# Layer 0's second FFN projection in three chunks, the last by column groups, with its weights' low parts on GpSimd

## The chip, the cores and the metric

One core of one Trainium2 chip runs the kernel. The metric is the device time of one execution in microseconds, as the median of several runs. Times inside an execution are counted from its first instruction.

## What is computed

A diffusion trunk of two layers over 256 context and 512 latent tokens (768 columns in all), model width 1024. Layer 0 has a mixer (pooling and a gated recurrence), layer 1 grouped-query attention; each is followed by a SwiGLU FFN with 2816 hidden units. Every sub-layer is wrapped in two RMSNorms and in a modulation (shift, scale, gate) that is computed from the conditioning vectors:

```python
def swiglu(h, w_in, w_out):
    a, b = jnp.split(h @ w_in, 2, axis=-1)
    return (jax.nn.silu(a) * b) @ w_out
...
        f_lat = swiglu(rmsnorm(x, norm_g[l, 2]) * (1.0 + sc2) + sh2, ffn_w_in[l], ffn_w_out[l])
        x = x + g2 * rmsnorm(f_lat, norm_g[l, 3])
...
        h_lat = rmsnorm(x, norm_g[l, 0]) * (1.0 + sc1) + sh1
```

The stretch of the kernel in question is `@ w_out` of layer 0, then its norm and residual (the "postnorm"), then the norm and modulation ahead of layer 1 (the "prenorm"), then the projection to queries and keys of layer 1 with RMSNorm per head and rotary positions.

## The kernel before

**Layout and products.** All activations are feature-major: 128 features in the partitions, tokens along the free axis; width 1024 is 8 tiles of 128. Every 32-bit product is made of three products of rounded parts, high by high, high by low and low by high (`mm3`, L185 to L187). A weight slot of 2048 columns is loaded as 1024-column pieces `raw` by SyncE's queue (L113, a pool of four buffers); ScalarE writes the high part (`whi`, `w3hi`, L641), and VectorE subtracts it to get the low part (`wlo`, `w3lo`, L642).

**The projection** (`ffn0`). The 22 hidden tiles of 128 went to DRAM (`gd`) while the first projection ran, and come back through GpSimd's DMA queue: `g` (L790) and `hh`/`hl` (L806). The 22 tiles are summed in four chunks of 7, 8, 3 and 4 (`FCH`). In the first three the loops run over the 8 output tiles n and, inside, over the column groups 0 to 256 and 256 to 768; the result of a chunk is added to `y` on VectorE (L734; the first chunk is copied by ScalarE, L732). The last chunk of 4 runs over three column groups of 256 instead (256 to 512, 512 to 768, then the context 0 to 256), and inside over n. All seven loads of `g` for the last two chunks, and before them the sixteen of the second chunk, are issued in one go.

**Work alongside.** A generator given to `along` is run in steps by `tick`: the code hands it as many microseconds of credit as the matmuls just written take, and a step costs what the generator yields. So the order of the code on each engine is set by these costs (VectorE, ScalarE and GpSimd run their queues in order). Beside the first three chunks the modulation of layer 1 is computed (`ada_cols`: 24 weight rows `adat`, each loaded as a `raw` and multiplied by the conditioning vector `cb` on VectorE, L366; twice for the first 16 rows). After each column group of the last chunk, `done` is started along the next: `postnorm` and `prenorm`, in steps for each of the 8 feature tiles: squares on ScalarE and their sums on VectorE (`ss`, L232, L233), the sum over partitions by TensorE (`rms`, L204), the power on GpSimd (`rr`, L210), the spread by TensorE (L219), the scaled tile `u` (L294, L249), the addition to `x` on GpSimd (L298), the high and low parts `hh`, `hl` (L256, L257).

**The projection to queries and keys** (`att_proj`) takes these `hh`, `hl`. First four heads of queries on the columns 256 to 512, two heads on 512 to 768, two more there, then both groups of keys, the other queries on 256 to 768, and the context's keys. Per head there is a sum of squares (`sq`, L912), a partition sum (L204), and the rotary positions (`sw`, L883 to L886, partition swaps by DMA). The first attention matmuls (`st`) follow.

Of the kernel before, what the change touches and what calls it, by code (L numbers as in the profile page):

```python
# [15 lines left out]
D = 1024  # L16
# [16 lines left out]
FCH = ((7, 8, 3, 4), (4, 4, 4, 4, 4, 2))  # L33
# [37 lines left out]

class Byg:
# [5 lines left out]
    def add(self, a, src):  # L78
        t = self.t[a // 256] = self.pool.tile([128, KD, 256], F32, tag=self.tag, name=self.tag, bufs=self.bufs)
        self.eng.dma_start(out=t, in_=src[:, :, a:a + 256])  # L80
        return t

    def __call__(self, k, a, b):
        return self.t[a // 256][:, k, a % 256:a % 256 + b - a]

# [7 lines left out]
class Trunk:  # L93
# [30 lines left out]
    def wtile(self, pool=None, tag="w"):  # L124
# [3 lines left out]
        return [pool.tile([128, 2048], F32R, tag=tag + t, name=tag + t) for t in ("hi", "lo")]  # L128
# [131 lines left out]

    def sumsq_all(self, xa):
# [21 lines left out]
    def postnorm(self, x, y, l, which, a, b):  # L283
# [8 lines left out]
        for k in range(KD):  # L292
# [6 lines left out]
            yield 0.75  # L299

# [58 lines left out]
    def ada_cols(self, m):  # L359
# [4 lines left out]
        for i in range(2 if m < 16 else 1):  # L364
            junk = self.rawp.tile([128, 1024], F32, tag="raw", name="junk") if m < 16 and not i else raw
            nc.vector.scalar_tensor_tensor(out=junk, in0=raw, scalar=1.0, in1=self.cb[:, i * 1024:i * 1024 + 1024],  # L366
                                           op0=ALU.mult, op1=ALU.mult, accum_out=self.mods[1][:, m, i:i + 1])
# [3 lines left out]
    def load_cb(self, cb, n):  # L371
        self.cb = cb
        self.nc.sync.dma_start(out=cb, in_=self.a["cb"][:n].partition_broadcast(128))
        self.nc.scalar.activation(out=cb, in_=cb, func=AF.Silu)
# [367 lines left out]
    def ffn0(self, y, h, closed, done, top):  # L742
# [18 lines left out]
        for i, (a, b) in [(i, g) for i in range(3) for g in G3[:2]] + [(i, G3[2]) for i in range(3)]:  # L761
            if a == G3[2][0] and i == 0:
# [4 lines left out]
                self.load_cb(self.tmp.tile([128, 1024], F32, name="cb0"), 1024)  # L767
# [19 lines left out]
        with self.pool("g2", side="right") as gp:  # L787
            def gload(j, k):
                t = gp.tile([128, 2, NT], F32R, tag=f"g{k}", name=f"g{k}")
                nc.gpsimd.dma_start(out=t, in_=gd[j].bitcast(F32R))  # L790
# [10 lines left out]
            with self.pool("cb") as cp:  # L801
                cb = cp.tile([128, 2048], F32, name="cb1")
                gb = self.htiles()
                for k in range(KD):
                    for p in range(2):
                        nc.gpsimd.dma_start(out=gb[p](k, 0, NT), in_=gd[7 + k][:, p, :].bitcast(F32R))  # L806
                g.append(gb)
                for ci in range(3):
                    if ci == 2:
                        ts = [gload(15 + k, k) for k in range(7)]  # L810
                        g += [two(ts[:3]), two(ts[3:])]
# [524 lines left out]
```

## Time and profile before

| | |
|---|---|
| median of 3 runs | 1622.92 us (1621.41 to 1623.31) |
| the profiled execution | 1618.92 us |
| its span, first to last instruction | 1617.2 us |
| TensorE busy in it | 1538.5 us (95%) |
| VectorE / ScalarE / GpSimd busy | 1001.6 / 644.2 / 120.9 us |
| second projection, from its first matmul to the first of the query projection | 768.7 to 962.0 us |
| query and key projection, up to the first `st` | 962.0 to 1067.9 us |
| mean granted TensorE clock | 0.985 of full speed |

The profile lists busy time of each engine, the idle time ahead of groups of instructions and what ended it. Matmuls overlap in the pipeline, so a matmul's own duration is longer than its pitch; times of stretches are read from starts. The median is 4.0 us above the profiled execution.

### The profile page before, as it was taken

Reading aid. Unit: us, or ns where it says so; the run is one execution under the profiler, and the core shown is the slowest. Engines: PE = TensorE matmul, PEld = TensorE weight load, DVE = VectorE, ACT = ScalarE, POOL = GpSimd, SP = SyncE. Lnnn points to the kernel's source line nnn. Section 1 sums busy time; section 2 is a strip of 40 time slices with the busy share of each in tenths; the row PEclk is TensorE's granted clock in tenths of the full one; section 3 lists DMA queues with packets and bytes.
Section 4 is the critical chain, followed back from the end, with each engine's and each line's share of the span. In section 5 each row is a group of like instructions: output and inputs, shape, how many; then the busy total and the mean of one; then the engine's idle time right before and its main releaser. Section 6 shows DMA issues by size and latency. Waiting matters only on the chain.

```text
span 1617.2 us, 26585 instructions
## 1 busy us (share of the span) xinstructions
PE 1538.5 (95%) x10656; PEld 1378.1 (85%) x10656; DVE 1001.6 (62%) x1923; ACT 644.2 (40%) x1228; POOL 120.9 (7%) x166
## 2 busy tenths in 40 slices
PE   5999999999899999999999996999998999999997
PEld 2877777789899999999888896899998988888886
DVE  5466575644779988974367476679947434244345
ACT  3334343254655444443221134458945332222222
POOL 0000000001210000001100022310013000000002
PEclk9999999999999999999999997999999999999999
DMA  9142232342415565536996322230032332332211
GB/s 368 55 157 80 79 128 83 124 134 89 154 64 175 193 194 192 170 127 237 354 319 210 100 87 81 77 97 27 1 118 66 105 101 83 103 104 89 94 53 52
DMA packets 75850, 207.25 MB, mean 128 GB/s; under 512 B 7760, under 2 KB 32848, under 8 KB 75600
## 3 DMA queue, kind: packets, MB, share of 16 engines
q1 hardware_dynamic: 70448, 184.92, 35.1%
q0 software_dynamic: 5136, 20.45, 3.4%
q8 instruction: 83, 1.36, 0.4%
q14 instruction: 39, 0.32, 0.1%
q10 hardware_dynamic: 144, 0.20, 0.0%
HBM read 178.28 MB, written 24.64 MB: 125 GB/s over the span
## 4 chain that ended last, share of the span: by engine, by line
PE 58%; DVE 6%; DMA 5%; ACT 2%; POOL 2%; issue 1%; SPq 0%; POOLq 0%; DVEq 0%; ACTq 0%
PE mm L185 18%; PE mm L186 18%; PE mm L187 18%; DMA gd<-gs 2%; DMA raw<-adat 1%; DVE ss L233 1%; PE pp L1024 1%; DMA raw<-w_fo 1%; POOL x L298 1%; PE aux L204 1%; PE st L185 1%; PE aux L219 1%; PE st L187 1%; PE st L186 1%; DVE wlo L642 1%
## 5 line engine op out<-in xcount | busy, mean ns | idle before, releaser
L185 PE MATMUL mm<-hh,whi 128*128 128x256 f32 (+2 forms) x1292 | 428.6, 334 | 5.0 <-DVE y L734 2.9
L187 PE MATMUL mm<-hh,wlo 128*128 128x256 f32 (+2 forms) x1292 | 425.5, 331 | 1.3 <-issue 1.0
L186 PE MATMUL mm<-hl,whi 128*128 128x256 f32 (+2 forms) x1292 | 425.9, 331 | 0.0
L185 PEld LDWEIGHTS mm<-hh,whi 128*128 128x128 f32 x1292 | 246.3, 192 | 34.9 <-issue 7.7
L187 PEld LDWEIGHTS mm<-hh,wlo 128*128 128x128 f32 x1292 | 246.5, 191 | 19.1 <-issue 1.2
L186 PEld LDWEIGHTS mm<-hl,whi 128*128 128x128 f32 x1292 | 246.7, 191 | 16.6 <-DVE hl L642 0.2
L641 ACT ACTIVATE whi<-raw 128x1024 fp32r<-128x1024 f32 (+2 forms) x145 | 133.9, 945 | 234.4 <-PE mm L186 122.7
L642 DVE TENSOR_TENSOR wlo<-raw,whi 128x1024 fp32r<-128x1024 f32 (+2 forms) x145 | 156.4, 1093 | 58.4 <-ACT whi L641 56.9
L210 POOL TENSOR_TENSOR rr<-rv,mhalf 128x2 f32<-128x2 f32 (+1 forms) x53 | 41.7, 789 | 1096.7 <-DVE rv L207 1078.7
L678 DVE TENSOR_TENSOR sa<-sa,mm 128x256 f32<-128x256 f32 (+2 forms) x38 | 20.7, 546 | 159.1 <-PE mm L187 159.0
L734 DVE TENSOR_TENSOR y<-y,mm 128x256 f32<-128x256 f32 (+1 forms) x104 | 55.9, 542 | 69.4 <-PE mm L187 68.5
L185 PE MATMUL mm<-hh,w3hi 128*128 128x256 f32 (+2 forms) x284 | 93.3, 330 | 2.8 <-ACT w3hi L641 1.4
L187 PE MATMUL mm<-hh,w3lo 128*128 128x256 f32 (+2 forms) x284 | 92.8, 327 | 1.4 <-DVE w3lo L642 1.4
L186 PE MATMUL mm<-hl,w3hi 128*128 128x256 f32 (+2 forms) x284 | 92.9, 328 | 0.0
L641 ACT ACTIVATE w3hi<-raw 128x1024 fp32r<-128x1024 f32 (+2 forms) x51 | 43.2, 876 | 101.7 <-PE mm L186 71.6
L233 DVE TENSOR_TENSOR ss<-ss,sq 128x256 f32<-128x256 f32 x126 | 58.0, 468 | 37.3 <-ACT sq L232 32.1
L366 DVE SCALAR_TENSOR_TENSOR raw<-raw,cb 128x1024 f32<-128x1024 f32 x48 | 58.7, 1222 | 12.4 <-DMA raw<-adat 11.7
L642 DVE TENSOR_TENSOR w3lo<-raw,w3hi 128x1024 fp32r<-128x1024 f32 (+2 forms) x51 | 50.1, 1001 | 16.4 <-ACT w3hi L641 16.4
L185 PEld LDWEIGHTS mm<-hh,w3hi 128*128 128x128 f32 x284 | 53.9, 190 | 6.5 <-ACT q L705 1.7
L187 PEld LDWEIGHTS mm<-hh,w3lo 128*128 128x128 f32 x284 | 53.8, 190 | 4.7 <-DVE w3lo L642 1.6
L186 PEld LDWEIGHTS mm<-hl,w3hi 128*128 128x128 f32 x284 | 53.9, 190 | 3.1
L185 PE MATMUL mm<-g,whi 128*128 128x256 f32 (+1 forms) x176 | 54.5, 310 | 0.0
(294 smaller groups left out, 3354.1 us busy)
## 6 DMA issues: line engine op xcount, KB each, us to landing
raw<-w_fi SPq DMA_DIRECT2D x88, 512.0 KB, 4.3
raw<-ada SPq DMA_DIRECT2D x48, 512.0 KB, 5.3
raw<-adat SPq DMA_DIRECT2D x48, 512.0 KB, 4.3
raw<-w_fo SPq DMA_DIRECT2D x40, 512.0 KB, 4.5
gd<-gs SPq DMA_DIRECT2D x38, 384.0 KB, 2.8
g<-gd POOLq DMA_DIRECT2D x14, 768.0 KB, 11.7
raw<-w_ab SPq DMA_DIRECT2D x20, 512.0 KB, 4.7
x<-x SPq DMA_DIRECT2D x6, 1024.0 KB, 6.9
```

The costliest lines, as they stand in the source:

```text
L185: self.nc.tensor.matmul(out=out, lhsT=wh, rhs=xh, start=first and i == 0, stop=False, **kw)
L186: self.nc.tensor.matmul(out=out, lhsT=wh, rhs=xl, start=False, stop=False, **kw)
L187: self.nc.tensor.matmul(out=out, lhsT=wl, rhs=xh, start=False, stop=i == n - 1, **kw)
L204: nc.tensor.matmul(out=pc[:, 2 * t:2 * t + 2], lhsT=ss[:, t * 128:(t + 1) * 128], rhs=self.ones[:, 0:2], start=True, stop=True)
L210: nc.gpsimd.tensor_tensor(out=r[:, :nt], in0=v[:, :nt], in1=self.mhalf[:, :nt], op=ALU.pow)
L219: nc.tensor.matmul(out=pb[:, t * 128:(t + 1) * 128], lhsT=r[:, t:t + 1].to_broadcast([128, 128]), rhs=self.ident, start=True, stop=True)
L233: nc.vector.tensor_tensor(out=ss[:, :n], in0=ss[:, :n], in1=sq[:, :n], op=ALU.add)
L366: nc.vector.scalar_tensor_tensor(out=junk, in0=raw, scalar=1.0, in1=self.cb[:, i * 1024:i * 1024 + 1024], op0=ALU.mult, op1=ALU.mult, accu ...
L641: self.nc.scalar.activation(out=hi, in_=src, func=AF.Copy)
L642: (eng or self.nc.vector).tensor_tensor(out=lo, in0=src, in1=hi.bitcast(F32), op=ALU.subtract)
L678: nc.vector.tensor_tensor(out=s[:, :n], in0=s[:, :n], in1=p[1][:, :n], op=ALU.mult)
L734: nc.vector.tensor_tensor(out=y(n, a, b), in0=y(n, a, b), in1=pt[:, :b - a], op=ALU.add)
```

## The change

- **Chunks.** 7, 8 and 7 hidden tiles. The first two run as before; the last, now 7 tiles, runs by the three column groups as the chunk of 4 did, with its own packing of weights (`w_fo0c`, 7168 columns in four slots; the fourth in a small pool `we`), and all are loaded before its first group.
- **Loads held.** `fetch` prepares a slot of weights one slot ahead. While it runs, low parts are computed on GpSimd (`weng`). The DMAs that bring `hh`/`hl` of the second chunk, `g` of the third and `x` are issued two tiles (or so) per slot; ahead of each, GpSimd copies two columns of the slot's last low part into the target, so that the DMA cannot start before that low part is there.
- **Modulation.** Rows 0 to 15 run beside the first two chunks, from the fourth output tile on, at a cost of 5.7 (before: all 24 from the fifth, at 5.0); rows 16 to 23 run beside the last chunk at 2.1. `cb` is two tiles of 1024, and the unused product has its own tile `junk` in place of a `raw`.
- **Norms.** `postnorm4` and `prenorm4` work on four feature tiles at once: squares of 128x1024 on ScalarE, sums of 512 columns, the scaling as one 128x1024 instruction from PSUM; the residual addition is one 128x1024 addition on GpSimd for tiles 0 to 3 and four fused multiply-adds on VectorE for tiles 4 to 7.
- **Query and key projection.** Keys of the first latent group follow its four query heads; then four heads of the second group, its keys, heads 4 to 6 on both, the context's keys, and head 7. Squares have their own buffers.

The core of the diff:

```diff
-FCH = ((7, 8, 3, 4), (4, 4, 4, 4, 4, 2))
+FCH = ((7, 8, 7), (4, 4, 4, 4, 4, 2))
...
+    def add(self, a, src, hold=None):
         t = self.t[a // 256] = self.pool.tile([128, KD, 256], F32, tag=self.tag, name=self.tag, bufs=self.bufs)
+        if hold is not None:
+            self.eng.tensor_copy(out=t[:, 0, 0:2], in_=hold)
         self.eng.dma_start(out=t, in_=src[:, :, a:a + 256])
...
+    def sumsq4(self, src, a, b):
+        nc = self.nc
+        ss = self.sm.tile([128, 256], F32, tag="ss", name="ss")
+        for k in (0, 4):
+            sq = self.np.tile([128, 4, 256], F32, tag="sq", name="sq", bufs=1)
+            nc.scalar.activation(out=sq, in_=src.view(a, b, k, k + 4), func=AF.Square)
+            nc.vector.tensor_tensor(out=sq[:, 0:2, :], in0=sq[:, 0:2, :], in1=sq[:, 2:4, :], op=ALU.add)
+            for x, z in ((sq[:, 0, :], sq[:, 1, :]),) if k == 0 else ((ss, sq[:, 0, :]), (ss, sq[:, 1, :])):
+                nc.vector.tensor_tensor(out=ss, in0=x, in1=z, op=ALU.add)
+            yield 1.3
...
+    def scaled(self, out, src, rb, a, b, k):
+        self.nc.vector.tensor_tensor(out=out.view(a, b, k, k + 4), in0=src.view(a, b, k, k + 4),
+                                     in1=rb[:, :b - a].unsqueeze(1).to_broadcast([128, 4, b - a]), op=ALU.mult)
...
+    def postnorm4(self, x, y, l, which, a, b):
...
+        for k0 in (0, 4):
+            self.scaled(y, y, rb, a, b, k0)
+            if k0 == 0:
+                for k in range(k0, k0 + 4):
+                    nc.scalar.activation(out=y(k, a, b), in_=y(k, a, b), func=AF.Copy,
+                                         scale=self.gcol[l][which][:, k, c:c + 1])
+                nc.gpsimd.tensor_tensor(out=x.view(a, b, 0, 4), in0=x.view(a, b, 0, 4), in1=y.view(a, b, 0, 4), op=ALU.add)
+            else:
+                for k in range(k0, k0 + 4):
+                    nc.vector.scalar_tensor_tensor(out=x(k, a, b), in0=y(k, a, b), scalar=self.gcol[l][which][:, k, c:c + 1],
+                                                   in1=x(k, a, b), op0=ALU.mult, op1=ALU.add)
+            yield 3.0
...
+                def fetch():
...
+                    ci, n = nxt.pop(0)
+                    w = wo[ci, n] = self.fo(0, ci, n)
+                    t = w[1][:, 1024:1026].bitcast(F32)
+                    if ci == 0:
+                        for k in (n, n + 1):
+                            for p in range(2):
+                                if n:
+                                    nc.gpsimd.tensor_copy(out=gb[p](k, 0, 2), in_=t)
+                                nc.gpsimd.dma_start(out=gb[p](k, 0, NT), in_=gd[7 + k][:, p, :].bitcast(F32R))
+                    elif n:
+                        for k in range(n - 2, n if n < 6 else 7):
+                            gl.append(gload(15 + k, k, t))
+                        if n == 6:
+                            x.add(256, self.x1, t)
...
+                self.weng = nc.gpsimd
+                fetch()
+                for ci in range(2):
                     for n in range(KD):
-                        if n % PER[FCH[0][ci]] == 0:
-                            wo = self.fo(0, ci, n)
+                        if n % 2 == 0:
+                            fetch()
...
-                        if (ci, n) == (0, 4):
-                            self.along("ada", ada1(0, 24, 5.0))
+                        if (ci, n) == (0, 3):
+                            self.along("ada", ada1(0, 16, 5.7))
...
+                wo = [self.wslot(self.a["w_fo0c"][i], 2048 if i < 3 else 1024, *(() if i < 3 else (we, "we"))) for i in range(4)]
+                self.along("ada", ada1(16, 24, 2.1))
+                x.add(512, self.x1, wo[2][1][:, 1024:1026].bitcast(F32))
+                for a, b in GL + GS[:1]:
+                    for n in range(KD):
...
+                        nc.vector.tensor_tensor(out=y(n, a, b), in0=y(n, a, b), in1=pt[:, :b - a], op=ALU.add)
+                        self.tick(2.24)
+                    self.along((a, 0), done(x, h1, a, b))
...
         for hd in range(4):
             queries(w[hd // 2], hd, *GL[0])
-        for hd in range(2):
-            queries(w[0], hd, *GL[1])
-        wk = self.wslot(self.a["w_at"][0], 2048)
-        for hd in range(2, 4):
-            queries(w[1], hd, *GL[1])
-        w.append(self.wslot(self.a["w_at"][3], 2048))
-        for g in GL:
-            keys(wk, *g)
+        wk = self.wslot(wa[0], 2048, w3, "w3")
+        keys(wk, *GL[0])
+        for hd in range(4):
+            queries(w[hd // 2], hd, *GL[1])
+            if hd % 2:
+                w.append(self.wslot(wa[3 + hd // 2], 2048))
+        keys(wk, *GL[1])
```

How the change moves instructions, at three places. First TensorE, around the norms of the columns 512 to 768. `aux<-ones,ss` is the partition sum of a postnorm or prenorm, `aux<-consts,rr` its spread, `aux<-ones,sq` a query head's sum, `mm` rows are the projections. Before, the postnorm's sum, its spread and the prenorm's sum:

```order
5138 L204 MATMUL aux<-ones,ss 128x2 x2
...
5144 L219 MATMUL aux<-consts,rr 128x128 x2
5145 L204 MATMUL aux<-ones,sq 128x2 x2
5146 L186 MATMUL mm<-hl_9278,whi 128x256
...
5156 L187 MATMUL mm<-hh_9273,wlo 128x256
5157 L204 MATMUL aux<-ones,sq 128x2 x2
5158 L204 MATMUL aux<-ones,ss 128x2 x2
5159 L219 MATMUL aux<-consts,rr 128x128 x2
```

Now, the same three:

```order
5068 L222 MATMUL aux<-ones,ss 128x2 x2
5069 L203 MATMUL mm<-g_8526,whi 128x256
...
5090 L237 MATMUL aux<-consts,rr 128x128 x2
5091 L203 MATMUL mm<-g_8526,whi 128x256
...
5192 L222 MATMUL aux<-ones,ss 128x2 x2
5193 L222 MATMUL aux<-ones,sq_9851 128x2 x2
5194 L205 MATMUL mm<-hh_9032,wlo 128x256
```

Between the spread and the prenorm's sum stood 11 matmuls of 256 columns; now there are 101, and the postnorm's sum and spread stand inside the last chunk (`mm<-g`), not inside the query projection.

Second, GpSimd at the start of the projection. Before, the second chunk's sixteen DMAs (rows 23 to 38) follow the first chunk's seven at once, and the third and fourth chunks' seven follow an `x`:

```order
15 L80 DMA x<-x_73 128x8x256
16 L790 DMA g_7885<-gd_4422 128x1536
...
22 L790 DMA g_7897<-gd_4428 128x1536
23 L806 DMA hh_8028<-gd_4429 128x768
...
38 L806 DMA hl_8043<-gd_4436 128x768
39 L80 DMA x<-x_73 128x8x256
40 L790 DMA g_9015<-gd_4437 128x1536
```

Now:

```order
15 L722 TENSOR_TENSOR w3lo<-raw,w3hi 128x1024
16 L722 TENSOR_TENSOR w3lo<-raw,w3hi 128x768
17 L722 TENSOR_TENSOR wlo<-raw,whi 128x1024
18 L873 DMA g_7878<-gd_4415 128x1536
...
28 L906 DMA hl_8035<-gd_4423 128x768
29 L722 TENSOR_TENSOR wlo<-raw,whi 128x768
30 L722 TENSOR_TENSOR wlo<-raw,whi 128x1024
31 L905 CAST hh_8028<-wlo 128x2
...
35 L722 TENSOR_TENSOR wlo<-raw,whi 128x768
36 L906 DMA hh_8028<-gd_4424 128x768
```

Three low parts now stand ahead of the first chunk's seven loads of `g`, and later loads stand behind low parts and two-column copies (CAST).

Third, VectorE at the start of the second chunk. L366 and L445 are products of the modulation, L734 and L814 add a group's sum from PSUM to `y`. Before:

```order
891 L366 SCALAR_TENSOR_TENSOR raw,mods_101<-raw,cb_8027 128x1024
892 L734 TENSOR_TENSOR y_3498<-y_3498,mm 128x256
893 L642 TENSOR_TENSOR w3lo<-raw,w3hi 128x1024 x2
894 L734 TENSOR_TENSOR y_3498<-y_3498,mm 128x512
895 L366 SCALAR_TENSOR_TENSOR junk,mods_101<-raw,cb_8027 128x1024
```

Now:

```order
860 L445 SCALAR_TENSOR_TENSOR raw,mods_101<-raw,cbx 128x1024
861 L814 TENSOR_TENSOR y<-y,mm 128x256
862 L445 SCALAR_TENSOR_TENSOR junk,mods_101<-raw,cb_8020 128x1024
863 L445 SCALAR_TENSOR_TENSOR raw,mods_101<-raw,cbx 128x1024
864 L445 SCALAR_TENSOR_TENSOR junk,mods_101<-raw,cb_8020 128x1024
865 L814 TENSOR_TENSOR y<-y,mm 128x512
```

The low parts have left VectorE's queue here; the additions to `y` still stand behind products that need a loaded row of the modulation.

## Rows read from the trace of the kernel before

**Rows 1.** The page's first part: busy time, share of the span, instructions of each engine.
```profile
PE 1538.5 (95%) x10656; PEld 1378.1 (85%) x10656; DVE 1001.6 (62%) x1923; ACT 644.2 (40%) x1228; POOL 120.9 (7%) x166
```
**Rows 2.** Waits of TensorE over the whole span: us in total, times, longest us.
```profile
PE aux L204 <- DVE ss L233: 23.7, 7, 12.8
...
PE mm L185 <- DVE y L734: 2.9, 1, 2.9
```
**Rows 3.** TensorE's timeline: start, us, what, and in brackets the idle time before.
```profile
772.00 0.39 PE L185 MATMUL mm<-g,w3hi 128*128 128x256 f32 x1 [0.16 <-DMA g<-gd]
...
851.06 0.50 PE L185 MATMUL mm<-hh,whi 128*128 128x512 f32 x1 [2.87 <-DVE y L734]
...
989.80 0.98 PE L204 MATMUL aux<-ones,ss 128*128 128x2 f32 x4 [12.84 <-DVE ss L233]
991.95 1.22 PE L219 MATMUL aux<-consts,rr 128*128 128x128 f32 x4 [1.16 <-POOL rr L210]
...
994.71 1.22 PE L185 MATMUL mm<-hh,whi 128*128 128x256 f32 x4 [0.91 <-ACT hh L256]
...
1027.25 0.98 PE L204 MATMUL aux<-ones,ss 128*128 128x2 f32 x4 [3.92 <-DVE ss L233]
```
**Rows 4.** Stretches: length; busy us of PE, PEld, DVE, ACT, POOL; clock, DMA share, GB/s.
```profile
768.70:828.49 59.79, 59.63 (x337) 51.61 (x337) 31.38 (x47) 15.64 (x26) 9.51 (x18) 1.00 0.93 315
828.49:899.96 71.47, 68.60 (x385) 60.26 (x384) 43.65 (x72) 8.64 (x12) 0.94 (x2) 0.98 0.75 260
...
981.19:998.26 17.07, 6.39 (x28) 6.25 (x29) 13.78 (x35) 7.05 (x17) 4.18 (x6) 0.50 0.24 77
1025.57:1032.39 6.82, 5.14 (x23) 4.98 (x23) 2.50 (x7) 3.11 (x8) 1.39 (x2) 0.50 0.00 0
851.49:854.90 3.41, 3.41 (x10) 2.66 (x9) 3.37 (x7) 0.00 (x0) 0.00 (x0) 0.50 0.46 129
1000.00:1020.00 20.00, 20.00 (x169) 19.86 (x169) 12.72 (x36) 8.64 (x18) 9.10 (x11) 1.00 0.36 104
```
**Rows 5.** The chain that ended last: the spread and next sum of columns 256 to 512.
```profile
943.28 0.45 PE aux L219 x4
...
955.24 0.34 PE aux L204 x4
```
**Rows 6.** GpSimd's timeline: the first chunk's loads, and two residual additions.
```profile
755.28 2.64 POOL L790 DMA_DIRECT2D g<-gd  x5 [0.84 <-DVE gs L642]
...
979.98 1.58 POOL L298 TENSOR_TENSOR x<-x,u 128x256 f32<-128x256 f32 x2 [1.69 <-DVE u L294]
```
**Rows 7.** VectorE's timeline: the same rotary product alone, and beside GpSimd's second addition.
```profile
978.62 0.42 DVE L885 TENSOR_TENSOR sw<-sw,sin 128x256 f32<-128x256 f32 x1
...
980.91 0.94 DVE L885 TENSOR_TENSOR sw<-sw,sin 128x256 f32<-128x256 f32 x1
```
**Rows 8.** Groups of instructions from 760 to 1070: busy us, mean ns, idle before.
```profile
L642 DVE TENSOR_TENSOR wlo<-raw,whi 128x1024 fp32r<-128x1024 f32 x25 | 30.4, 1222 | 6.3 <-ACT whi L641 6.3
...
L249 DVE SCALAR_TENSOR_TENSOR u<-x,scol,aux 128x256 f32<-128x256 f32 x24 | 10.7, 475 | 2.6 <-PE aux L219 2.6
...
L298 POOL TENSOR_TENSOR x<-x,u 128x256 f32<-128x256 f32 x24 | 19.3, 832 | 12.6 <-DVE u L294 12.6
...
L641 ACT ACTIVATE whi<-raw 128x1024 fp32r<-128x1024 f32 x26 | 27.0, 1058 | 74.5 <-DMA raw<-w_fo 37.7 <-PE mm L186 36.8
L256 ACT ACTIVATE hh<-u,mods 128x256 fp32r<-128x256 f32 x24 | 11.2, 504 | 12.9 <-DVE u L249 12.9
```
**Rows 9.** The chain that ended last, ahead of the wait at 851.
```profile
837.59 10.48 DMA raw<-w_fo
...
850.33 0.69 DVE y L734
```
**Rows 10.** The page's DMA issues: KB each, median us from issue to landing.
```profile
raw<-adat SPq DMA_DIRECT2D x48, 512.0 KB, 4.3
...
g<-gd POOLq DMA_DIRECT2D x14, 768.0 KB, 11.7
```

More of the change, by code (lines that the diff above doesn't have):

```diff
@@ L259, in prenorm, with prenorm4 @@
             yield 0.8
+    def sumsq4(self, src, a, b):
[8 more added lines that the diff above has]
+            yield 1.3
+        yield Y1
+        return ss
+    def scaled(self, out, src, rb, a, b, k):
+        self.nc.vector.tensor_tensor(out=out.view(a, b, k, k + 4), in0=src.view(a, b, k, k + 4),
+                                     in1=rb[:, :b - a].unsqueeze(1).to_broadcast([128, 4, b - a]), op=ALU.mult)
+    def prenorm4(self, x, h, l, which, a, b, y):
+        nc = self.nc
+        n, c = b - a, int(b <= CTX)
+        ss = yield from self.sumsq4(x, a, b)
+        r = self.rms(ss, n, D)
+        yield LAG
+        rb = self.spread(r)
+        yield 1.0
+        for k0 in (0, 4):
+            self.scaled(y, x, rb, a, b, k0)
+            for k in range(k0, k0 + 4):
+                nc.scalar.activation(out=y(k, a, b), in_=y(k, a, b), func=AF.Identity,
+                                     scale=self.scol[l][which][:, k, c:c + 1], bias=self.shcol(l, which, k, c))
+            yield 1.8
+            for k in range(k0, k0 + 4):
+                self.split(h[0](k, a, b), h[1](k, a, b), y(k, a, b))
+            yield 1.8
     def sumsq_all(self, xa):
@@ L787, in ffn0, with gload @@
         with self.pool("g2", side="right") as gp:
-            def gload(j, k):
+            def gload(j, k, hold=None):
                 t = gp.tile([128, 2, NT], F32R, tag=f"g{k}", name=f"g{k}")
+                if hold is not None:
+                    nc.gpsimd.tensor_copy(out=t[:, 0, 0:2], in_=hold)
                 nc.gpsimd.dma_start(out=t, in_=gd[j].bitcast(F32R))
@@ L800, in ffn0 @@
             gsp.__exit__(None, None, None)
-            with self.pool("cb") as cp:
-                cb = cp.tile([128, 2048], F32, name="cb1")
+            cbp = self.pool("cb")
+            cb = cbp.__enter__().tile([128, 1024], F32, name="cb1")
+            with self.pool("cbx") as cp:
+                cbx = cp.tile([128, 1024], F32, name="cbx")
+                self.junk = cp.tile([128, 1024], F32, name="junk")
                 gb = self.htiles()
-                for k in range(KD):
-                    for p in range(2):
-                        nc.gpsimd.dma_start(out=gb[p](k, 0, NT), in_=gd[7 + k][:, p, :].bitcast(F32R))
@@ L807, in ffn0 @@
                 g.append(gb)
[L808 to L811, printed above, removed]
+                nxt = [(ci, n) for ci in range(2) for n in range(0, KD, 2)]
+                wo, gl = {}, []
+                def fetch():
+                    if not nxt:
+                        return
+                    ci, n = nxt.pop(0)
[12 more added lines that the diff above has]
+                            x.add(256, self.x1, t)
@@ L830, in ffn0 @@
+            cbp.__exit__(None, None, None)
         self.w3 = None
@@ L1132, in layer0 @@
             x = Byg(xpool.__enter__(), "x", 3, nc.sync)
[L1133 removed]
+            y = Whole(yp, KD, F32, "y")
             for s, _ in G3:
@@ L1145, in done @@
             def done(x, h1, s, e):
-                x.add(s, self.x1)
-                yield 0.1
-                yield from self.postnorm(x, y, 0, 1, s, e)
-                yield from self.prenorm(x, h1, 1, 0, s, e)
+                if s < CTX:
+                    x.add(s, self.x1)
+                    yield 0.1
+                yield from self.postnorm4(x, y, 0, 1, s, e)
+                yield from self.prenorm4(x, h1, 1, 0, s, e, y)
                 if s >= CTX:
```

76 lines of the change are left out of this document (49 added, 27 removed).

## The prediction

> **What bounds the kernel now.** I read the page's busy times first: TensorE works 1538.5 of 1617.2 us [rows 1], so work on another engine counts only where TensorE waits for it or runs at a lower clock. TensorE's waits come second: its largest is for a norm's sum of squares on VectorE (`ss`), 23.7 us in seven waits [rows 2]. TensorE's timeline places them, and around this projection they are few: 2.87 us at 851 for an addition to `y`, then 12.84, 1.16 and 0.91 us around 990, then 3.92 us at 1027 [rows 3]. That is 21.7 us. Third come stretches at a granted clock of 0.50, the lower of the two levels (1.2 of 2.4 GHz): 3.41 us after the wait at 851, 17.07 us around the one at 990, 6.82 us around the one at 1027, with 3.41, 6.39 and 5.14 us of matmuls in them [rows 4]. At the full clock these 14.9 us would take half: 7.5 us are lost. So some 29.2 us between 769 and 1068 are neither work nor full clock, and that is what this change can win; the rest is matmuls at their pace.
>
> **The norms.** The wait of 12.84 us is an effect of order. Before, the prenorm's sum for the columns 512 to 768 stands 11 matmuls behind the spread of the postnorm it depends on. A matmul of 256 columns has a pitch of 20.00/169 = 0.118 us [rows 4], so TensorE has 1.3 us of work there, and the chain between needs far more: for the columns 256 to 512 it ran from 943.28 to 955.24, 12.0 us [rows 5], behind 96 matmuls that covered it. Now 101 matmuls stand there, 11.9 us, and for the columns 256 to 512 it is 84, 9.9 us.
>
> What the new chain needs, from its steps: a scaling of 128x1024 (nearest row: VectorE's 128x1024 subtraction, 1.22 us), four scalings on ScalarE (0.50 each, 2.0), one addition of 128x1024 on GpSimd, then two squares of 128x1024 (1.06 each) and a last sum of 512 and two of 256 columns (0.6 and 2 x 0.42 us) [rows 7, 8]. Nothing in the trace is an addition of 128x1024 on GpSimd: four of its 128x256 additions take 4 x 0.83 = 3.3 us, VectorE's whole one 1.22 us [rows 8]. I take the upper end, since it is the same engine and operation. Sum: 1.22 + 2.0 + 3.3 + 2.1 + 1.4 = 10.1 us; with the lower end 8.0. VectorE's share for the other four tiles (1.22 + 4 x 0.475 = 3.1 us) runs beside GpSimd's. So the latent groups fit within a microsecond, 11.9 against 10.1 and 9.9 against 10.1. For the context, 96 matmuls of 256 and 26 of 512 columns stand between, 17.6 us, against about 15 before (119 and 4). I put 1 us of waiting here, between 0 and 7 (a wait and its half clock as at 1027, 3.92 + 2.6).
>
> **The matmuls.** Chunks of 3 and 4 tiles become one of 7: the same matmuls, but the 512-column ones of the chunk of 3 (8 x 9 = 72) become 144 of 256. In the first chunk, 168 of each width take 59.79 us [rows 4], so one of 512 takes (59.79 - 168 x 0.118)/168 = 0.238 us, twice 0.118. This costs nothing, at most 1 us by the rounding of these pitches. The additions to `y` fall by eight of 256 and eight of 512 columns.
>
> **The weights' low parts.** Sixteen subtractions leave VectorE for GpSimd. VectorE was busy 31.38 of 59.79 us in the first chunk and 43.65 of 71.47 in the second [rows 4], so its gain is only worth something where an addition to `y` waits behind other work, as at 851: there a low part waited for a load that took 10.48 us, and the addition stood behind it [rows 9]. On GpSimd a low part lies between 1.22 us and 3.3 us as above. Per slot of weights TensorE has 59.79/4 = 14.9 us. GpSimd has two low parts (6.6 at the upper end), up to four copies (0.8 at most, nearest the 128x256 addition) and four DMA issues (2.64/5 = 0.53 each [rows 6]): 6.6 + 3.3 + 2.1 = 12.0 us, below 14.9 and fetched a slot ahead. It is hidden. The cover gone, each microsecond more per slot is a microsecond of TensorE.
>
> Two prices come with it. First, three low parts now stand ahead of the seven loads of the first chunk, 3.4 to 9 us of GpSimd. The wait of 0.16 us at 772 shows that one of these loads came only just in time [rows 3], while five of the seven were issued from 755.28 on [rows 6]. An `x` of 1 MB no longer goes ahead of them (2.6 us at 400 GB/s), so I take 1.5 us of waiting, between 0 and 6. Second, GpSimd and VectorE disturb each other: a rotary product of 0.42 us took 0.94 us while a GpSimd addition ran [rows 6, 7]. By the Trainium skill, "SBUF — State Buffer", section "Who interferes with whom", a VectorE instruction with two SBUF inputs and a GpSimd instruction that reads SBUF exclude each other, the second to issue waiting for the first; the row agrees, 0.52 us longer. The modulation's products are of this kind, the additions to `y` (one input in PSUM) are not. If each of 16 low parts held up VectorE fully, that would be 16 x 3.3 = 53 us over 131 us in which VectorE had 75 us of work, of which 16 x 1.2 = 19 leave: 109 us, still under 131. So VectorE keeps room on average, but not at every addition.
>
> The skill's "GPSIMD Engine Reference", section 3.1, has a two-input elementwise instruction about twice as slow on GpSimd as on VectorE at 2048 columns, 4497 against 2293 ns; an estimate by it is 2.4 us for 1024, inside my bounds, which would make the chain of the norms 9.2 us and the slot 10.2.
>
> **The loads and the modulation.** Held loads spread the traffic; they move no bytes away. Loads on GpSimd's queue took 11.7 us, rows of the modulation 4.3 in the median [rows 10]. At 851 seven loads of `g` had just been issued together. Now two go per slot, so a late row is less likely; 16 instead of 24 rows compete with the additions to `y`, and 8 move beside the last chunk, where VectorE gets 8 x 1.22 = 9.8 us more of 504 x 0.118 = 59.5 us. I expect the 2.87 us and its half clock to go, and put 1.2 us (0 to 5) on what remains of such waits, since additions to `y` still stand behind products that wait for a load.
>
> **The query projection.** Keys and queries change places, with the same matmuls. The rotary chains no longer mix with the postnorm of 512 to 768, which is over by then.
>
> **Sum.** 29.2 - 1.0 - 1.5 - 1.2 = 25.5 us gained. Against the profiled execution that is 1618.92 - 25.5 = 1593.4 us; the median stands 4.0 us above it, so against the median 1622.92 I expect **1597.4 us**.
>
> **The rivals.**
> *Norms still late.* If the chain keeps the 12.0 us of [rows 5] or more, because additions to `y`, products of the modulation and rotary work come between, it is 2 us late at each of the latent groups, and the half clock comes with it. Two waits as at 1027 (3.92 + 2.6 us each) make 13 us: 1610. For it: VectorE gets the modulation's last third there. Against it: fewer and longer instructions, and nine times the distance.
> *Additions to `y` late again.* One or two waits as at 851, each 2.87 + 1.7 = 4.6 us: 1602 to 1607. For it: the order on VectorE is much the same, and a row's buffer comes free only after a low part on GpSimd.
> *GpSimd sets the pace: slower.* The slot's 12.0 us above lack the waits inside GpSimd's queue: it works in order, so a load held for a low part, or a low part that VectorE blocks, delays the next slot. If a low part takes 5 us under contention, a slot needs 10 + 3.3 + 2.1 = 15.4 us, more than 14.9, and each following slot comes later. From there the weights are late at most slots; at 3 us and 1.7 us of half clock for eight slots that is 38 us, less the 25.5: 1635. For it: GpSimd has hardly any work now (120.9 us in all [rows 1]). Against it: 5 us is well above both bounds, and the second chunk has 17 us per slot.
> *The change does little*, since waits reappear one place later (a later spread or the first `st`), equal to the gain: 1622.
>
> **How the numbers follow.** The likeliest course, at 1597.4 with 1591 to 1601 as its own range (all of the 29.2 us and 2 more; the costs at some 8 us), has 0.55. Additions late has 0.14, norms late 0.15, GpSimd's pace 0.10, no change 0.06. The range reaches from 1591 to 1611 and takes in the first three with a little left out. A measurement of this kernel can tell 0.2% (3.2 us) from no change. Faster by more than that: 0.84; within it: 0.06; slower: 0.10.
>
> **What would show it.** Right: no wait of TensorE for `ss` over 2 us between 769 and the first `st`; no stretch at a clock of 0.50 around the query projection; the first `st` near 1042; GpSimd's 128x1024 instructions between 1.2 and 3.3 us. Wrong: waits for GpSimd's low parts at the start of slots, a wait of several us for `g` near 772, or waits for `y` in the second chunk that grow.

## The result, and the profile after

The changed kernel takes **1636.31 us** (median of 4 runs, 1633.65 to 1637.53) beside 1623.12 us for the kernel before: a ratio of 1.008, with an interval of 1.0062 to 1.0097. It is 13 us slower where 25.5 us less were forecast. One experiment below, with the change's chunks, holds, norms and order and five corrections, takes 1597.12 us.

The stretches view of the changed kernel: first chunk, second chunk, last chunk, query and key projection, the rest (columns as in [rows 4]):

```profile
771.42:838.51 67.09, 62.93 (x338) 53.89 (x337) 35.66 (x39) 16.74 (x26) 36.51 (x38) 0.95 0.80 278
838.51:924.95 86.44, 72.80 (x385) 63.43 (x384) 38.25 (x56) 9.79 (x10) 16.70 (x16) 0.90 0.56 198
924.95:989.34 64.39, 63.36 (x530) 63.18 (x528) 43.30 (x78) 22.07 (x36) 8.33 (x8) 1.00 0.41 137
989.34:1079.93 90.59, 84.16 (x571) 78.68 (x569) 66.73 (x174) 48.59 (x107) 22.60 (x25) 0.92 0.36 103
1079.93:1634.30 554.37, 531.67 (x3122) 475.65 (x3121) 280.05 (x517) 220.20 (x395) 28.93 (x36) 0.98 0.23 75
```

| stretch, us | before | after | all corrections |
|---|---|---|---|
| up to the first matmul of the projection | 768.7 | 771.4 | 774.4 |
| first chunk | 59.8 | 67.1 | 59.4 |
| second chunk | 71.5 | 86.4 | 66.7 |
| rest of the projection, queries and keys | 167.9 | 155.0 | 147.3 |
| from the first `st` to the end | 549.3 | 554.4 | 549.9 |

The part meant to win does win, 12.9 us. The first chunk loses 7.3, the second 15.0, and the rest, which the change hardly seems to touch, 5.1 us. The first row of the table is not the change: TensorE's instructions are those of before, and the kernel before itself, with one number changed behind this stretch (the slot counter, below), took 774.3 us for it; over the profiled executions of this study it lasted between 767 and 776 us. The profiled execution of the kernel before also lies 4.2 us under its median, which is why the rows differ by 17 us in sum and the medians by 13. So profiles are compared by stretch here, and kernels by their medians.

TensorE's waits in the changed kernel, for comparison with [rows 2]:

```profile
PE mm L203 <- DVE y L814: 13.6, 3, 6.2
...
PE mm L203 <- ACT w3hi L721: 5.3, 3, 2.0
PE aux L222 <- DVE ss L288: 4.8, 3, 2.1
PE mm L203 <- DMA g<-gd: 4.2, 4, 1.9
```

The wait of 12.8 us for `ss` is gone. In its place TensorE waits 13.6 us for additions to `y` in the second chunk (2.9 before), 4.2 us for `g`, 3.9 of the 5.3 us for `w3hi` in layer 1, and still 4.8 us for the new norms' sums. VectorE's timeline shows why the additions are late:

```profile
772.95 4.86 DVE L722 TENSOR_TENSOR gs<-sa,gs 128x384 fp32r<-128x384 f32 x1 [0.70 <-ACT gs L721]
...
814.92 3.25 DVE L445 SCALAR_TENSOR_TENSOR raw<-raw,cbx 128x1024 f32<-128x1024 f32 x1
...
818.10 1.21 DVE L445 SCALAR_TENSOR_TENSOR junk<-raw,cb 128x1024 f32<-128x1024 f32 x1
...
857.86 1.23 DVE L445 SCALAR_TENSOR_TENSOR junk<-raw,cb 128x1024 f32<-128x1024 f32 x1 [4.41 <-DMA raw<-adat]
...
860.28 0.41 DVE L814 TENSOR_TENSOR y<-y,mm 128x256 f32<-128x256 f32 x1
865.62 3.29 DVE L445 SCALAR_TENSOR_TENSOR junk<-raw,cb 128x1024 f32<-128x1024 f32 x1 [4.92 <-DMA raw<-adat]
...
871.34 0.68 DVE L814 TENSOR_TENSOR y<-y,mm 128x512 f32<-128x512 f32 x1
```

A product of the modulation takes 1.2 us, or 3.3 when a low part runs on GpSimd; and it starts late, since it waits for its row (4.41 and 4.92 us here). The additions stand behind it. In the second chunk only two products are stretched, to 3.35 and 3.29 us; the waits for rows come to 22.6 us (8.36, 4.41, 4.92, 0.80 and 4.15). GpSimd's timeline over the same time:

```profile
773.23 4.12 POOL L722 TENSOR_TENSOR wlo<-raw,whi 128x768 fp32r<-128x768 f32 x2
...
805.98 1.21 POOL L905 CAST hl<-w3lo 128x2 fp32r<-128x2 f32 x1
...
811.34 5.74 POOL L722 TENSOR_TENSOR wlo<-raw,whi 128x1024 fp32r<-128x1024 f32 x2 [0.78 <-ACT whi L721]
...
865.48 2.34 POOL L722 TENSOR_TENSOR wlo<-raw,whi 128x1024 fp32r<-128x1024 f32 x1 [2.79 <-ACT whi L721]
```

A low part of 128x1024 takes 2.34 us in the single one at 865, where VectorE's product waits, and 2.87 each in the pair at 811. Beside the pair at 773 VectorE's low part of 128x384 took 4.86 us instead of 0.56.

### The profile page after: what moved, and what is told of

Read it like the earlier page. It is cut to its first block, busy times and chain, and to the rows that moved or that the text cites. A ratio compares the mean times of both kernels' runs of the same rounds, so it can differ in the third digit from the quotient of the medians.

```text
span 1634.3 us, 26615 instructions
## 1 busy us (share of the span) xinstructions
PE 1549.2 (95%) x10728; PEld 1391.0 (85%) x10728; DVE 994.0 (61%) x1854; ACT 652.7 (40%) x1228; POOL 158.9 (10%) x182
## 5 line engine op out<-in xcount | busy, mean ns | idle before, releaser
L203 PE MATMUL mm<-hh,whi 128*128 128x256 f32 (+2 forms) x1164 | 387.2, 334 | 13.6 <-DVE y L814 13.6
L205 PE MATMUL mm<-hh,wlo 128*128 128x256 f32 (+2 forms) x1164 | 383.7, 330 | 1.5 <-issue 1.2
L204 PE MATMUL mm<-hl,whi 128*128 128x256 f32 (+2 forms) x1164 | 384.2, 330 | 0.0
L203 PEld LDWEIGHTS mm<-hh,whi 128*128 128x128 f32 x1164 | 223.7, 192 | 40.5 <-DVE y L814 14.5
L204 PEld LDWEIGHTS mm<-hl,whi 128*128 128x128 f32 x1164 | 224.3, 193 | 13.6 <-DVE hl L722 0.2
L722 DVE TENSOR_TENSOR wlo<-raw,whi 128x1024 fp32r<-128x1024 f32 (+1 forms) x131 | 140.2, 1087 | 61.2 <-ACT whi L721 60.6
L203 PE MATMUL mm<-hh,w3hi 128*128 128x256 f32 (+2 forms) x412 | 140.6, 342 | 7.9 <-ACT w3hi L721 5.3
L205 PE MATMUL mm<-hh,w3lo 128*128 128x256 f32 (+2 forms) x412 | 139.0, 339 | 1.4 <-DVE w3lo L722 1.4
L204 PE MATMUL mm<-hl,w3hi 128*128 128x256 f32 (+2 forms) x412 | 139.1, 339 | 0.0
L814 DVE TENSOR_TENSOR y<-y,mm 128x256 f32<-128x256 f32 (+1 forms) x64 | 36.9, 585 | 63.1 <-PE mm L205 62.9
L203 PE MATMUL mm<-ghl,whi 128*128 128x512 f32 (+1 forms) x192 | 71.4, 375 | 0.0
L204 PE MATMUL mm<-gll,whi 128*128 128x512 f32 (+1 forms) x192 | 70.6, 373 | 0.0
L205 PE MATMUL mm<-ghl,wlo 128*128 128x512 f32 (+1 forms) x192 | 70.4, 372 | 0.0
L445 DVE SCALAR_TENSOR_TENSOR junk<-raw,cb 128x1024 f32<-128x1024 f32 x16 | 26.4, 1650 | 51.1 <-DMA raw<-adat 34.9
```

The source lines that it names most:

```text
L203: self.nc.tensor.matmul(out=out, lhsT=wh, rhs=xh, start=first and i == 0, stop=False, **kw)
L204: self.nc.tensor.matmul(out=out, lhsT=wh, rhs=xl, start=False, stop=False, **kw)
L205: self.nc.tensor.matmul(out=out, lhsT=wl, rhs=xh, start=False, stop=i == n - 1, **kw)
L722: (eng or self.nc.vector).tensor_tensor(out=lo, in0=src, in1=hi.bitcast(F32), op=ALU.subtract)
L814: nc.vector.tensor_tensor(out=y(n, a, b), in0=y(n, a, b), in1=pt[:, :b - a], op=ALU.add)
```

## Experiments

Theories: **G**, GpSimd's low parts are at fault for the second chunk, by way of VectorE's products; **L**, the order of loads in SyncE's queue is; **P**, the counter that hands out weight slots is at fault for layer 1; **M**, the place of `g` in memory is at fault for the first chunk. Those on the held loads (H), the norms (X) and the ring of the four `raw` buffers (R) came later.

**Low parts back on VectorE.**

```diff
-                self.weng = nc.gpsimd
                 fetch()
```

> All low parts of the weights back on VectorE; held loads, prefetch, chunks, norms and modulation as changed. Theory G (GpSimd's low parts block VectorE's two-input products, 3.3 in place of 1.22 us, and stand ahead of the first chunk's loads): the products all take 1.2 us, no wait for g over 0.5 us near 772 to 779, and the 13.6 us of waits for y in the second chunk fall below 4: about 16 to 22 us faster, 1614 to 1620. Theory L (a row of the modulation comes late because its load stands in SyncE's queue behind a weight load that waits for a buffer, and products ahead of the addition wait for it): only the first chunk's part goes, about 7 us, 1629, and waits for y of over 9 us stay.

1613.82 us (1611.36 to 1619.81), ratio 0.9946 (0.993 to 0.9962): 22.5 us below the changed kernel, and already faster than before. The two chunks, then the products' groups in the changed kernel and in this one:

```profile
775.82:841.32 65.50, 62.46 (x338) 53.70 (x337) 32.37 (x48) 16.99 (x27) 8.97 (x24) 0.95 0.87 300
841.32:908.04 66.72, 66.72 (x385) 59.05 (x384) 37.87 (x60) 9.58 (x11) 4.46 (x12) 1.00 0.69 237
```

```profile
L445 DVE SCALAR_TENSOR_TENSOR junk<-raw,cb 128x1024 f32<-128x1024 f32 x16 | 26.4, 1650 | 51.1 <-DMA raw<-adat 34.9 <-ACT cb L454 16.2
```

```profile
L445 DVE SCALAR_TENSOR_TENSOR junk<-raw,cb 128x1024 f32<-128x1024 f32 x16 | 19.6, 1224 | 38.7 <-DMA raw<-adat 21.1 <-ACT cb L454 17.6
```

The second chunk has no wait left: 66.72 us, all of it matmuls. As many products stand ahead of each of the first additions as in the changed kernel (24, then 27), so their order isn't at fault. What differs is the pace of the products and how late their rows are. These are the products that started at 857.86 and 865.62 in the changed kernel:

```profile
847.25 1.23 DVE L445 SCALAR_TENSOR_TENSOR junk<-raw,cb 128x1024 f32<-128x1024 f32 x1 [1.63 <-DMA raw<-adat]
...
855.62 1.23 DVE L445 SCALAR_TENSOR_TENSOR junk<-raw,cb 128x1024 f32<-128x1024 f32 x1 [3.27 <-DMA raw<-adat]
```

For the same products that made 22.6 us there, VectorE waits 10.6 us for rows here. For the second chunk G holds: which engine makes the low parts decides. L falls as a cause of its own. The first chunk keeps most of its loss, against G.

**Only the first slot's low parts on VectorE.**

```diff
-                self.weng = nc.gpsimd
                 fetch()
+                self.weng = nc.gpsimd
```

> Only the first slot's low parts (and so those ahead of the first chunk's loads of g) on VectorE, the other seven slots on GpSimd. Theory G and L both: loads of g leave some 6 us earlier, the waits for g (4.2 us in all) and the half clock behind them go: some 7 us faster, 1629; the waits for y in the second chunk stay at 10 us or more. Rival (these loads are late because of the traffic, not of GpSimd): no change, 1636.

1635.98 us (1630.55 to 1637.56): no change, as the rival had it.

```profile
771.54:837.01 65.47, 62.65 (x338) 53.99 (x337) 31.33 (x39) 16.85 (x26) 34.79 (x37) 0.95 0.82 284
837.01:924.21 87.20, 73.53 (x385) 63.96 (x384) 38.23 (x56) 9.80 (x10) 16.68 (x16) 0.90 0.57 195
```

The run moves less than was expected of it: of the three low parts ahead of the loads of `g`, two belong to the first slot, and the third stays. GpSimd's timeline:

```profile
756.08 2.40 POOL L722 TENSOR_TENSOR wlo<-raw,whi 128x1024 fp32r<-128x1024 f32 x1 [297.34 <-DMA raw<-w_fo]
758.44 3.97 POOL L873 DMA_DIRECT2D g<-gd  x7
```

The first load left 11.7 us ahead of the first matmul in the changed kernel, 13.1 us here, and 14.7 us with no low part on GpSimd; the first chunk took 67.09, 65.47 and 65.50 us. So the low parts are a small part of what makes these loads late, at most 1.6 us of it.

**No modulation in the first two chunks.**

```diff
-                            self.along("ada", ada1(0, 16, 5.7))
+                            nc.vector.memset(self.mods[1][:, 0:16, :], 0.0)
+                            self.ada_tail(1, 0, 8, self.mods[1][:, 0:8, :])
+                            self.ada_tail(1, 8, 16, self.mods[1][:, 8:16, :])
```

> The changed kernel with its low parts on GpSimd, but rows 0 to 15 of layer 1's modulation are left out (set to zero), with their loads. Theory G1 (the second chunk waits because VectorE's products, blocked by GpSimd's low parts and fed late, stand ahead of the additions to y): the 13.6 us of waits for y go, the second chunk takes 67 us, about 1617. Theory G2 (GpSimd's low parts themselves are late, so that weights come late): TensorE waits at the start of slots, now for w lo, some 10 us remain, 1627 or more.

1615.34 us (1614.12 to 1617.19), and the second chunk:

```profile
839.03:905.74 66.71, 66.71 (x385) 59.06 (x384) 17.39 (x26) 9.57 (x10) 13.98 (x16) 1.00 0.52 171
```

G1: with all low parts on GpSimd, the weights are never late. What cost time was the products that stand ahead of the additions. The run takes out the products together with the loads of their rows, so it doesn't separate these two.

**The last chunk, norms and query projection alone.** The first two chunks as before:

```diff
+                for k in range(KD):
+                    for p in range(2):
+                        nc.gpsimd.dma_start(out=gb[p](k, 0, NT), in_=gd[7 + k][:, p, :].bitcast(F32R))
...
-                self.weng = nc.gpsimd
-                fetch()
...
-                            self.along("ada", ada1(0, 16, 5.7))
+                            self.along("ada", ada1(0, 16, 5.0))
```

> Chunks 7, 8 and 7 with the last by column groups, new norms, new query projection and 16 and 8 rows of modulation stay; the first two chunks are written as in the kernel before: no held loads, no prefetch, low parts on VectorE, modulation from the fifth tile at a cost of 5.0. Theories G and L: the first two chunks take 60 and 67 to 72 us in place of 67 and 86; 1614 to 1619, faster than the kernel before. Rival (the last chunk and the norms bring nothing, the gain of 13 us seen there comes from work that the first chunks took over): no faster than 1623.

1626.17 us (1621.43 to 1629.56), ratio 1.0014 (1.0001 to 1.0027): neither came out as expected. The time is the rival's, but not its reason: the later stretches win their 12.9 us. G and L had put it at 1614 to 1619, but the second chunk takes 82.46 us, even with low parts on VectorE, and the first one 63.36:

```profile
858.47 0.58 PE L203 MATMUL mm<-hh,whi 128*128 128x256 f32 x1 [10.02 <-DVE y L814]
```

So additions to `y` come late without low parts on GpSimd, too. Here 30 products stand ahead of the first addition, not 24, and one row, issued at 835.50 behind seven loads of `g` in a burst, took 10.53 us to land.

**Prefetch without the holds.** Low parts on VectorE, and:

```diff
-                                if n:
-                                    nc.gpsimd.tensor_copy(out=gb[p](k, 0, 2), in_=t)
...
-                            gl.append(gload(15 + k, k, t))
+                            gl.append(gload(15 + k, k))
```

> Low parts on VectorE, and none of the two-column copies that hold a load back: the loads are issued as soon as their memory is free; the weights are still prepared one slot ahead. Theory H (holding keeps the modulation's rows and weights from standing behind a burst of g loads): waits for y of 8 us or more in the second chunk come back, with their half clock, 1626 to 1631. Rival (being a slot ahead is what helped, not the holding): as with the holds, 1612 to 1616.

1627.91 us (1623.48 to 1629.9): H. The same order on VectorE, but bursts of `g`:

```profile
859.59 0.58 PE L203 MATMUL mm<-hh,whi 128*128 128x256 f32 x1 [7.53 <-DVE y L814]
```

So holding the loads is worth 14 us by the medians, and the low parts on GpSimd cost more than that. In the two chunks of the profiles it is 7.6 us, 12.2 us won in the second and 4.6 lost in the first: without the holds the first chunk is nearly as short as before.

```profile
774.31:835.23 60.92, 59.80 (x338) 51.60 (x337) 31.91 (x47) 16.64 (x27) 9.52 (x18) 1.00 0.91 317
```

**The slot counter.** `wtile` gives every third weight slot to the pool `w3`. The change makes one slot fewer in the projection and gives another (`wk`) its pool by name, so layer 1 starts two counts lower. In the changed kernel:

```diff
         self.sb = SB2
+        self.nw += 2
```

> Two more numbers in the counter that hands every third weight slot to the extra pool w3, ahead of layer 1, so that layer 1's slots fall into the pools as in the kernel before. Theory P (the change shifted that counter, and the first FFN slot of layer 1 lost its buffer): the waits of 1.82 and 2.04 us for w3hi at 1241 and 1243 go, with the half clock behind them; about 5 us faster, 1631, nothing else moves. Rival (layer 1 starts later for another reason, as ScalarE is late): no change, 1636.

1628.29 us (1623.52 to 1631.48), 8 us less; the stretch from `st` to the end takes 550.2 us (554.4), and its two waits are gone. The other way round, in the kernel before (`self.nw += 1` at the same place):

> The kernel before, with one number more in the slot counter ahead of layer 1 and nothing else. Theory P (the counter alone costs the two waits for w3hi): the same two waits of 1.8 and 2.0 us appear at the start of layer 1's FFN, 4 to 6 us slower than before. Rival: no change.

1629.11 us (1625.67 to 1635.28), ratio 1.0035 (1.0021 to 1.005), and the waits stand there. TensorE's timeline of this run, then of the changed kernel:

```profile
1238.52 0.39 PE L185 MATMUL mm<-hh,w3hi 128*128 128x256 f32 x1 [1.82 <-ACT w3hi L641]
1241.06 0.58 PE L185 MATMUL mm<-hh,w3hi 128*128 128x256 f32 x1 [2.04 <-ACT w3hi L641]
```

```profile
1240.81 0.39 PE L203 MATMUL mm<-hh,w3hi 128*128 128x256 f32 x1 [1.82 <-ACT w3hi L721]
...
1243.35 0.39 PE L203 MATMUL mm<-hh,w3hi 128*128 128x256 f32 x1 [2.04 <-ACT w3hi L721]
```

P is shown from both sides: one number costs 6 to 8 us by the medians, 160 us behind the last instruction that the change moves. With the low parts on VectorE as well:

> Low parts on VectorE and the slot counter shifted, nothing else: the common base of the runs with the reverse allocation (1609.8) and with the postnorm's addition on VectorE (1601.5). Theories P and G as they stand: the two gains add, 22.5 from the low parts and 5 to 8 from the counter, 1606 to 1609, with waits for g of some 3 us and the norms' waits of 1.0, 2.1, 1.7 us, none for y over 1 us. Rival (the gains overlap): 1613.

1606.65 us (1605.4 to 1612.88): the two gains add (22.5 and 8.0 would give 1605.8).

**The tiles of `g` in reverse.** On that base, to test M (`gtile` only allocates a tile, `gload` then loads it):

```diff
-            g = [two([gload(j, j) for j in range(7)])]
+            first = {k: gtile(k) for k in reversed(range(7))}
+            g = [two([gload(j, j, None, first[j]) for j in range(7)])]
```

> Low parts on VectorE and the slot counter shifted for layer 1 (together some 1609 if the two runs before add up), and the seven tiles of g allocated in reverse, so that the tile loaded first no longer lies on memory that VectorE frees late. Theory M (the new norm buffers moved g onto such memory; its first load left 3.6 us later than before and all others behind it): the first load leaves up to 6 us earlier relative to the first matmul that needs it, no wait for g above 0.5 us, half clock gone: 1602 to 1604. Rival (the traffic at that place makes them late): no change, 1609.

1609.81 us (1604.73 to 1610.66): no gain, and yet the first chunk does what M says. GpSimd's timeline of the base, then of this one:

```profile
753.49 0.73 POOL L873 DMA_DIRECT2D g<-gd  x1 [298.00 <-ACT gs L721]
```

```profile
751.87 0.73 POOL L876 DMA_DIRECT2D g<-gd  x1 [292.12 <-PE mm L205]
752.79 2.14 POOL L876 DMA_DIRECT2D g<-gd  x4 [0.18 <-issue]
```

The first load now leaves 20.7 us ahead of the first matmul of the projection, 14.8 in the base (19.1 in the kernel before), and the first chunk takes 59.36 us without a wait, 65.66 in the base. But the place in memory isn't the only condition: in the run without the holds the first load left 15.0 us ahead as well, and the chunk took 60.92 us. What else decides stays open. And the second chunk gives the gain back:

```profile
772.56:831.92 59.36, 59.36 (x338) 51.70 (x337) 32.44 (x48) 17.48 (x29) 7.63 (x21) 1.00 0.82 283
831.92:904.36 72.44, 68.58 (x386) 60.28 (x385) 38.48 (x60) 9.68 (x11) 5.77 (x16) 0.98 0.69 238
```

```profile
855.49 0.50 PE L203 MATMUL mm<-hh,whi 128*128 128x512 f32 x1 [3.86 <-DVE y L814]
```

59.36 + 72.44 = 131.8 us, beside 65.66 + 67.52 = 133.2 without it. TensorE came earlier to a place where the modulation's rows set the pace; the last run below tests this.

**The postnorm's addition wholly on VectorE.** On the same base, eight fused multiply-adds, no GpSimd addition, no scalings on ScalarE:

```diff
-            if k0 == 0:
...
-                nc.gpsimd.tensor_tensor(out=x.view(a, b, 0, 4), in0=x.view(a, b, 0, 4), in1=y.view(a, b, 0, 4), op=ALU.add)
-            else:
-                for k in range(k0, k0 + 4):
+            for k in range(k0, k0 + 4):
```

> Low parts on VectorE, slot counter shifted (some 1609 as the two runs before add up), and the residual addition of the new postnorm wholly on VectorE (eight fused multiply-adds, no GpSimd addition, no four scalings on ScalarE). Theory X (GpSimd's addition of 2.4 us blocks VectorE's fused multiply-adds, 3.4 us for three in place of 1.4, and lengthens the chain): the waits for ss (1.0, 2.1, 1.7 us) halve or go with the half clock behind them, 1601 to 1606. Rival (the chain is set by the two squares through one buffer and by weights' low parts that stand between its sums): waits stay within 0.7 us, 1608 to 1610.

1601.45 us (1600.88 to 1607.26), 5.2 us less. The runs of the two kernels overlap (the base has 1605.4 to 1612.88), but the stretch from the last chunk to the first `st` agrees, 147.5 us beside 153.4. The time is X's; its reason is shown in part. What stood there, with low parts on VectorE (its timeline, then ScalarE's), and then here:

```profile
970.71 3.40 DVE L376 SCALAR_TENSOR_TENSOR x<-y,gcol,x 128x256 f32<-128x256 f32 x3
974.03 1.21 DVE L722 TENSOR_TENSOR wlo<-raw,whi 128x1024 fp32r<-128x1024 f32 x1
```

```profile
978.88 1.06 ACT L285 ACTIVATE sq<-x 128x1024 f32<-128x1024 f32 x1 [2.22 <-DVE ss L288]
```

```profile
965.78 1.67 DVE L370 SCALAR_TENSOR_TENSOR x<-y,gcol,x 128x256 f32<-128x256 f32 x4
```

Three took 3.40 us beside GpSimd's addition, four take 1.67 without it. From the spread to the prenorm's sum of the columns 512 to 768 it was 14.8 us and is 14.1. So the chain itself is only 0.7 us shorter. The wait of 2.1 us went also because the steps' credits now put 113 matmuls between the two, not 101, 1.4 us more of work at 0.118 us each; the run doesn't separate these two.

**All together, and the modulation spread wider.** The four corrections together, then also the modulation's steps at a higher cost:

> Everything that helped, together: low parts on VectorE, slot counter shifted, g allocated in reverse, residual addition of the postnorm wholly on VectorE. Theory R (in the second chunk the ring of four raw buffers sets the pace: a product frees a buffer, a load of 4 to 7 us fills it, and the additions to y stand behind the products; starting 6 us earlier only makes TensorE wait there): a wait for y of 3 to 4 us near 855 stays, 1599 to 1603, as without the reverse allocation (1601.5). Rival (the wait at 855 in the run with the reverse allocation was chance): both gains add, 1595 to 1597.

1600.48 us (1599.55 to 1603.27), with a second chunk of 72.41 us: R, the rows' pace again, and the reverse order of `g` gains nothing that shows on the run before.

```diff
-                            self.along("ada", ada1(0, 16, 5.7))
+                            self.along("ada", ada1(0, 16, 6.6))
```

> As best, with the modulation's steps at a cost of 6.6 in place of 5.7, so that about two products fewer stand ahead of each of the first additions to y in the second chunk. Theory R: the additions no longer wait for the ring, wait at 855 below 1.5 us, 1595 to 1598. Rival (the products that are late move to the next additions or to the last chunk and make TensorE wait there): within 2 us of best.

**1597.12 us** (1594.04 to 1599.48), ratio 0.9831 (0.9814 to 0.9848). Four products fewer stand ahead of the first addition of the second chunk, and nothing waits there. The four stretches of the projection and the queries:

```profile
774.37:833.73 59.36, 59.36 (x337) 51.69 (x337) 29.80 (x44) 17.47 (x29) 8.98 (x24) 1.00 0.81 281
833.73:900.45 66.72, 66.72 (x385) 59.05 (x384) 40.68 (x64) 9.67 (x10) 7.31 (x12) 1.00 0.76 258
900.45:963.92 63.47, 63.36 (x530) 63.18 (x528) 41.10 (x81) 20.07 (x30) 4.14 (x6) 1.00 0.41 136
963.92:1047.79 83.87, 79.63 (x571) 74.26 (x569) 67.21 (x184) 46.44 (x101) 21.37 (x24) 0.98 0.36 111
```

## Why the prediction was wrong

**The step that failed most is that on the weights' low parts.** It asked whether GpSimd keeps up, found 12.0 of 14.9 us per slot and called it hidden; and whether VectorE keeps room on average, 109 of 131 us. Both are true (no weight was late), and neither decides. What decides is a ring: a product frees a `raw` buffer, SyncE's queue then loads the next row or weights into it, and the next product waits for that load, while the additions to `y` stand between products in a fixed order. GpSimd's low parts can lengthen the ring twice: products took 1.65 us on average in place of 1.22, and a buffer waits for a low part of 2.3 to 2.9 us. The row at 851 [rows 3, 9] had shown this ring at its limit, and the sum put 1.2 us (0 to 5) on it. It was 13.6 us of waits and 72.80 - 66.72 = 6.1 us of half clock (granted clock 0.90 in the stretch, 1.00 with the low parts on VectorE), 19.7 us. How the loss divides is open; no run here separates the two. SyncE's own waits speak for the first: between 760 and 925 us, 15 of them (72.6 us) end with a product and none with a low part of GpSimd. A third part may be the loads themselves: a row took 6.8 us to land in the median of the second chunk (835 to 890), 4.5 with the low parts on VectorE (841 to 905).

By the Trainium skill, "SBUF — State Buffer", section "Who interferes with whom", the second of two such instructions waits for the whole of the first. The products at 3.25 and 3.29 us agree, 1.22 and most of a low part. I had used the rule for an average over 131 us; its effect is on single instructions. The estimate by the Trainium skill's "GPSIMD Engine Reference", section 3.1, of 2.4 us for 1024 columns was right, 2.34 us; my upper end of 3.3 us was too long, which did no harm.

**The norms: mechanism right, the term mis-sized.** The wait of 12.84 us went as reasoned. The chain was put at 10.1 us against a room of 11.9, and is 14.8: the fused multiply-adds ran beside GpSimd's addition (3.40 us for three), four low parts for the query weights stand ahead of and between the sums (4.8 us), and the second square waits for the sums of the first, since they share one buffer. I had counted the two squares as consecutive and taken VectorE's half as free beside GpSimd's. In place of 1.0 us the stretch from the last chunk to the first `st` lost 11.7: it took 155.0 us against an ideal of 167.9 - 18.8 - 5.8 = 143.3. These are waits (4.8 us for `ss`, 2.6 for the spreads' `rr`) and half clock.

**The loads of `g`: size and cause wrong.** The 1.5 us for GpSimd's low parts ahead of them were 7.7 us (67.09 against 59.36), and these low parts were at most 1.6 us of it. With these on VectorE, the rest goes when the tiles of `g` are allocated in reverse: the first tile lay on memory that is freed late. Most of it also goes without the holds (60.92 us), so the place in memory is not the only condition. That it is the new norm buffers (one `sq` of four tiles, no `u`) that moved the tile is argued from the code, not isolated.

**Not foreseen at all: the slot counter**, 5.1 us in the stretch (4.2 of them came back in the run that shifts it), in a part of the program I had taken as unchanged because its instructions are the same in kind and number.

Together these four are 18.5 + 10.7 + 6.2 + 5.1 = 40.5 us above the sum's terms; the median came out 38.9 us above the forecast.

**Right:** the matmuls cost nothing more (with the four corrections, at the full clock, TensorE is busy 141.7 us from the last chunk to the first `st`, beside 147.9 - 5.8 = 142.1 before), the holds help (14 us), and the query projection's new order has no wait for `ss` over 2.1 us. Two of the three named signs of being wrong came, the wait for `g` and the growing waits for `y`. Of the rivals, "GpSimd sets the pace" gave the time that came, 1635, by a mechanism that did not (late weights), which is luck; "additions to `y` late again" gave the mechanism, down to the buffer that waits for a low part, at less than half its size. That all corrections together end at the forecast's 1597 is chance as well: they are another kernel.

## What to carry to other kernels

When work moves to another engine, don't ask whether that engine has room: follow the buffers it frees, and who stands in order behind the one that waits for them; here a ring already at its limit turned the delay into 19.7 us. Look for side effects of an edit on shared state, such as slot counters and where buffers lie, before calling the rest of the program unchanged. And a gain ahead of such a ring is given back at it until the ring itself is relieved.

## What the runs showed that was not expected

- A short VectorE instruction can wait for more than one GpSimd instruction: 4.86 us for a 128x384 subtraction (0.56 alone) beside two GpSimd low parts that ran back to back for 4.12 us.
- It goes the other way too: GpSimd's copies of 128x2 took about 0.18 us, but up to 1.21 us beside VectorE's products.
- TensorE's same instructions ahead of this projection took 767 to 776 us in different profiled executions, so a single profile can't judge a change of 0.5%.
